# Two extra PSUM banks for the first eight projections of a hybrid mixer, and a modulation round whose end is cut into three steps

## The chip, the core and the metric

The kernel runs on one core of a Trainium2 chip. The metric is the device time of one execution in microseconds, from the first instruction to the last, as the median of several runs. The engines are named as in the profile: PE is TensorE (PEld its weight loads), DVE is VectorE, ACT is ScalarE, POOL is GpSimd, SP is the engine whose queue starts most DMAs.

## What is computed

Two blocks of two layers each, over 512 tokens of width 1024 with a context of 256 tokens, all in float32. The first block has a spatial gate and a two-way recurrent mixer in its first layer, a chunked matrix-memory mixer in its second, and a convolutional feed-forward part in both; what enters and leaves each part is scaled and shifted by a modulation, six vectors of 1024 for each layer, computed from a condition vector:

```python
def ada_mod(cvec, w, b):
    m = jax.nn.silu(cvec) @ w + b
    m = m.reshape(cvec.shape[:-1] + (6, D_MODEL))
...
```

The second block, run twice, is the hybrid mixer. One projection is split into many parts; q, k and v go through a short convolution, q and k are normalised, and four heads run a gated delta rule in chunks of 64 tokens in both directions; beside that a branch with a convolution of 31 taps, and two gates that mix the branches:

```python
def hybrid_mixer(h, w_in, qkv_conv_w, a_log, ...):
    proj = h @ w_in
    qkv, z_a, a_lg, b_lg, cf_val, cf_glu, z_b, gate_lg = jnp.split(proj, pts, axis=-1)
    qkv = jax.nn.silu(depthwise_conv_centred(qkv, qkv_conv_w))
    q = l2_normalize(q)
    k = l2_normalize(k)
    ...
    o_fwd = gated_delta_chunked(q, k, v, g[:, :, 0], beta[:, :, 0])
    o_bwd = flip(gated_delta_chunked(flip(q), flip(k), flip(v), ...))
    ...
    y = gate[:, :, 0] * y_a + gate[:, :, 1] * y_b
    return y @ w_out
```

## The kernel before

**Matmuls.** A float32 product is made of three fp32r matmuls for each of eight blocks of 128 rows: the weight tile is split into a high part `wh` (ACT, line 77) and a low part `wl` (DVE, line 78), the input likewise beforehand, and lines 329, 332 and 333 multiply high with high, high with low and low with high. One tile of 128 output columns over 512 tokens is thus 24 matmuls of 128x512 into one PSUM bank. Raw weights come by DMA into a ring of two buffers (`wr`); the split tiles have rings of three.

**PSUM banks.** An `Env` holds lists of bank numbers; `K.mm()` takes the next bank of `env.mm`, `K.ps()` the next of `env.ps`, each list in rotation. The main environment has 0 to 3 for `mm` and 4 to 7 for `ps`. A bank is one buffer: whoever takes it waits until the last reader of its previous content is done, in the order of the program's text.

**Strands.** `K.background` hands a generator to a list; at every `yield a, b` a strand is put off by a nominal time `b`, and `tick`, called between the matmuls of the main text, runs a step of each strand that is due. The text order so made is then reordered engine by engine by the framework's scheduler. Of the PE instructions of a step only the first is pinned behind the first of the step before it. The order on each engine is fixed when the program is built, and each engine runs its list in order.

**A hybrid.** `hybrid(K, CH, l, X)` first computes the gate rows (`gate_rows`, one tile of 24 matmuls), their cumulated sums `gc` along chunks (line 1809), and brings them into columns: `columns` transposes with four PE instructions each (line 1443) into a `ps` bank and copies (line 1446). There are four such columns, in this text order: `gcT`, `egT`, `beT`, `kdT`; then `eglT` (PE line 1833, copy line 1836). These five take consecutive banks of the main `ps` list: 5, 6, 7, 4, 5 in the first hybrid, and 6, 7, 4, 5, 6 in the second (counted from the program's calls of `K.ps()`).

After them in the text come the projections. `proj(h)` calls `gdn_proj`, which makes four tiles of 24 matmuls: k, q, v and za of head h, below called k0, q0, v0, za0, k1 and so on. The bank of k, q and v is read by one ACT instruction (line 1770) and four DVE instructions (line 1778). k and q are then passed through Silu (line 1996) and Square (line 1999), and the sum of squares goes through PE (`ps<-ones,qsq`, line 359, four instructions), DVE (line 349), POOL (line 351) and PE again (line 371). `pro` is the environment of the projections with the `mm` banks 0, 1 and 2, so that za0 takes the bank of k0, k1 that of q0, and so on. Two strands `head(0)` and `head(1)` have the `ps` banks 4, 5 and 6, 7; `head(0)` begins after `proj(0)`, `head(1)` after `proj(1)`. Then follow `cf_proj`, the strand `cf_conv`, `proj(2)`, `proj(3)` and the gates.

In the trace, the matmuls of all these tiles have lines 329, 332 and 333; the program's order, printed further down, tells the tiles apart by number.

**The modulation rounds.** `ada_steps` computes 2048 columns of the modulation in one round: eight steps, each with two or three loads into `wr` buffers (or, every third step, into the rings of `wh` and `wl`) and four matmuls of 32x512 (line 539), then a copy `adav` out of PSUM (DVE, line 545), four PE transposes (line 548) and two DVE additions (line 553). Its `ps` list is bank 3 alone. Round 0 runs at the start; five rounds run as one strand beside the strands of the recurrent mixer in the first layer, and then beside that mixer's output projection (`gemm_out`, weights `ab_w_out`).

Of the kernel before, what the change touches and what calls it, by code (L numbers as in the profile page):

```python
# [81 lines left out]
class Kern:  # L82
# [431 lines left out]
    def ada_steps(self, layer, rounds):  # L514
        nc = self.nc
        w = self.ins["ada_w"]
        if not hasattr(self, "mod"):
            self.mod = {}
            cs = self.const([P, KD, 32], name="csil")
            nc.gpsimd.memset(cs, 0.0)  # L520
            for i, key in enumerate(("c", "c_ctx")):
                nc.scalar.activation(cs[:, :, i], self.vt[key], AF.Silu)
            self.csil = cs
        if layer not in self.mod:
            self.mod[layer] = self.const([P, 2, 48], name="mod")
        mod = self.mod[layer]
        for r in rounds:
            ps = self.ps()
            for k in range(KD):
                if k % 3 < 2:  # L530
                    raw = self.wpool.tile([P, 2048], F32, tag="wr", bufs=2, name=self.nm("ar"))
                    raw = [raw[:, :1024], raw[:, 1024:]]
                else:
                    raw = [self.wpool.tile([P, 1024], F32, tag=t, bufs=3, name=self.nm("ar")) for t in ("wh", "wl")]
                for h in range(2):
                    c0 = 2048 * r + 1024 * h
                    self.lines[mybir.EngineType.SP] = nc.sync.dma_start(raw[h], w[layer, k * P:(k + 1) * P, c0:c0 + 1024]).ins
                for c in range(4):
                    m = nc.tensor.matmul(ps[32 * c:32 * c + 32, :], self.csil[:, k, :],  # L539
                                         raw[c // 2][:, 512 * (c % 2):512 * (c % 2) + 512], start=k == 0, stop=k == KD - 1)  # L540
                    if self.back and c == 0:
                        self.tc.keep_in_program_order(m)
                yield 860, ADL
            ev = self.p2(name="adav")
            nc.vector.tensor_copy(ev, ps)
            pt = self.ps()
            for q in range(4):
                nc.tensor.transpose(pt[:, q * P:(q + 1) * P], ev[:, q * P:(q + 1) * P], self.ident)
            self.free(ev)
            bias = self.vt[f"ada_b{layer}"]  # L550
            for i in range(2):
                src = pt.rearrange("p (q c x) -> p c q x", q=4, c=4)[:, :, :, i]
                nc.vector.tensor_tensor(mod[:, i, 16 * r:16 * r + 16].rearrange("p (c q) -> p c q", c=4), src,
                                        bias[:, 16 * r:16 * r + 16].rearrange("p (c q) -> p c q", c=4), ADD)
# [1227 lines left out]
def hybrid(K, CH, l, X):  # L1782
# [56 lines left out]
    pro = Env([0, 1, 2], [3], [], range(16, 24))  # L1839
    heads = [Env([], (4 + 2 * a, 5 + 2 * a), range(7 * a, 7 * a + 7), range(8 * a, 8 * a + 8)) for a in range(2)]  # L1840

    def proj(h):
        pre[h] = gdn_proj(K, l, h, X, w)

    def head(a):
        pads = CH.pads(K.p2)
        for h in (a, a + 2):
            while h not in pre:
                yield 0, 2000
            yield from gdn_head(K, CH, l, h, *pre.pop(h), gcT, ngT, beT, bkT, eglT, gcd, egd, Ya, pads)  # L1850
        K.free(*pads)

    K.env = pro
    K.gk = GKH
    for e in heads:
        K.lend([e], p=HP)
    for h in range(2):
        proj(h)
        K.background(heads[h], head(h), slow=SLG)
    cf_proj(K, l, X, w, U)  # L1860
    conv = cf_conv(K, l, U)
    K.background(pro, conv)
# [426 lines left out]
```

## Time and profile before

| what | value |
|---|---|
| median of 3 runs | 3439.56 us (3436.07 to 3442.67) |
| profiled execution | 3440.7 us, span 3439.0 us |
| PE busy | 3202.1 us, 93% of the span |
| DVE, ACT, POOL busy | 2121.8, 1272.1, 628.5 us |
| mean granted TensorE clock | 0.952 |
| chain that ended last, by engine | PE 78%, DVE 11%, ACT 3%, DMA 3% |

The first hybrid runs from about 2267 us to 2840 us of the span, the second from about 2846 us to the end; the five background rounds of the modulation lie between 400 and 770 us. A line of the timeline is: start, duration, engine, line, operation, output<-inputs, shapes, count, and in brackets the time for which the engine stood idle before it and whose end ended that. A matmul's duration overlaps the next one's, so a stretch is measured from start to start.

### The profile page before, as it was taken

Reading aid. Unit: us, or ns where it says so; the run is one execution under the profiler, and the core shown is the slowest. Engines: PE = TensorE matmul, PEld = TensorE weight load, DVE = VectorE, ACT = ScalarE, POOL = GpSimd, SP = SyncE. Lnnn points to the kernel's source line nnn. Section 1 sums busy time; section 2 is a strip of 40 time slices with the busy share of each in tenths; the row PEclk is TensorE's granted clock in tenths of the full one; section 3 lists DMA queues with packets and bytes.
Section 4 is the critical chain, followed back from the end, with each engine's and each line's share of the span. In section 5 each row is a group of like instructions: output and inputs, shape, how many; then the busy total and the mean of one; then the engine's idle time right before and its main releaser. Section 6 shows DMA issues by size and latency. Waiting matters only on the chain.

```text
span 3439.0 us, 62780 instructions
## 1 busy us (share of the span) xinstructions
PE 3202.1 (93%) x25436; PEld 2523.3 (73%) x25436; DVE 2121.8 (62%) x4341; ACT 1272.1 (37%) x2679; POOL 628.5 (18%) x762
## 2 busy tenths in 40 slices
PE   7999988989799999989988999979999898999998
PEld 5878767767588888868766788857767576766766
DVE  4444555645755555585765675667587656777665
ACT  4343343333442222355524332352333335234332
POOL 4111232311000000010010000005158000516600
PEclk9999998989899999999998999989999899999979
DMA  6432454441221222222222233232222253223233
GB/s 231 138 91 70 150 161 142 141 135 52 69 71 63 74 66 68 74 67 79 86 69 86 86 108 113 87 98 71 72 92 96 77 176 93 70 68 101 96 107 114
DMA packets 313573, 336.15 MB, mean 98 GB/s; under 512 B 26542, under 2 KB 259132, under 8 KB 313284
## 3 DMA queue, kind: packets, MB, share of 16 engines
q1 hardware_dynamic: 311172, 329.69, 30.2%
q8 instruction: 200, 3.28, 0.4%
q0 software_dynamic: 2112, 2.45, 0.3%
q14 instruction: 89, 0.73, 0.1%
HBM read 282.13 MB, written 49.94 MB: 97 GB/s over the span
## 4 chain that ended last, share of the span: by engine, by line
PE 78%; DVE 11%; ACT 3%; DMA 3%; issue 2%; POOL 2%; SPq 0%; DVEq 0%; POOLq 0%; ACTq 0%
PE mm L329 20%; PE mm L332 18%; PE mm L333 18%; PE ps L720 2%; PE ps L1176 2%; PE ps L729 2%; DVE cfa L1778 2%; PE ps L1121 1%; PE ps L539 1%; PE ps L371 1%; PE ps L2128 1%; DVE wl L78 1%; PE ps L1703 1%; PE ps L2115 1%; PE ps L2142 1%
## 5 line engine op out<-in xcount | busy, mean ns | idle before, releaser
L329 PE MATMUL mm<-hl,wh 128*128 128x512 f32 (+1 forms) x3296 | 1250.0, 383 | 42.8 <-DVE qkv L1778 15.0
L332 PE MATMUL mm<-hl,wh 128*128 128x512 f32 (+1 forms) x3296 | 1220.1, 371 | 1.1 <-DVE hl L468 0.8
L333 PE MATMUL mm<-hl,wl 128*128 128x512 f32 (+1 forms) x3296 | 1212.7, 370 | 0.0
L329 PEld LDWEIGHTS mm<-hl,wh 128*128 128x128 f32 x3296 | 628.2, 191 | 184.2 <-issue 38.2
L333 PEld LDWEIGHTS mm<-hl,wl 128*128 128x128 f32 x3296 | 628.3, 191 | 113.0 <-issue 2.5
L332 PEld LDWEIGHTS mm<-hl,wh 128*128 128x128 f32 x3296 | 630.0, 191 | 103.0 <-issue 2.8
L77 ACT ACTIVATE wh<-wr 128x512 fp32r<-128x512 f32 (+3 forms) x718 | 368.0, 562 | 694.1 <-PE mm L332 600.3
L78 DVE TENSOR_TENSOR wl<-wr,wh 128x512 fp32r<-128x512 f32 (+3 forms) x718 | 439.3, 645 | 221.5 <-ACT wh L77 205.2
L1356 DVE SCALAR_TENSOR_TENSOR cv<-mm,vecs,cv 128x441 f32<-128x441 f32 (+2 forms) x352 | 243.4, 692 | 93.6 <-ACT cv L1344 87.2
L1407 POOL MEMSET gwh<- 128x1024 f32 x3 | 2.9, 955 | 964.5 <-PE mm L332 964.5
L1778 DVE SCALAR_TENSOR_TENSOR cfa<-ld,vecs,cfa 128x497 f32<-128x497 f32 (+14 forms) x160 | 152.3, 952 | 18.1 <-ACT cfa L1772 16.0
L1944 POOL TENSOR_SCALAR tap<-ld,vecs 128x498 f32<-128x498 f32 (+4 forms) x80 | 146.5, 1831 | 50.7 <-DVE kq L2003 12.4
L1379 DVE TENSOR_TENSOR fy<-fy,mm 128x512 f32<-128x512 f32 x96 | 55.2, 577 | 126.2 <-PE mm L333 125.5
L1945 POOL TENSOR_TENSOR cfa<-cfa,tap 128x498 f32<-128x498 f32 (+4 forms) x80 | 119.1, 1489 | 5.5
L2120 ACT ACTIVATE u<-ps,beT 64x128 f32<-64x128 f32 x128 | 46.5, 363 | 152.6 <-DVE u L2119 151.6
L724 ACT ACTIVATE pad<-ps 128x256 f32<-128x256 f32 (+1 forms) x100 | 46.7, 467 | 150.9 <-PE ps L720 147.9
L1358 ACT ACTIVATE cv<-cv,vecs 128x256 f32<-128x256 f32 (+1 forms) x66 | 43.2, 654 | 132.7 <-DVE cv L1356 78.1
L351 POOL TENSOR_TENSOR rs<-var,mhalf 128x4 f32<-128x4 f32 (+1 forms) x26 | 29.0, 1115 | 287.7 <-DVE var L349 287.6
L406 PE MATMUL ps<-sq,one 128*128 128x512 f32 (+1 forms) x132 | 64.0, 625 | 18.9 <-ACT sq L376 17.2
L730 DVE TENSOR_TENSOR cut<-cut,ps 128x256 f32<-128x256 f32 x120 | 49.3, 415 | 51.4 <-PE ps L729 49.9
L1362 DVE TENSOR_TENSOR cv<-cv,mm 128x512 f32<-128x512 f32 x66 | 39.5, 599 | 65.5 <-ACT cv L1358 35.4
L2119 DVE TENSOR_SCALAR u<-ps,kdT 64x128 f32<-64x128 f32 x128 | 44.7, 349 | 52.1 <-PE ps L2115 41.8
(476 smaller groups left out, 4578.9 us busy)
## 6 DMA issues: line engine op xcount, KB each, us to landing
ar<-in_ada_w_dram SPq DMA_DIRECT2D x96, 512.0 KB, 4.8
wr<-in_ffn_up_dram SPq DMA_DIRECT2D x44, 1024.0 KB, 5.1
wr<-in_w_in_dram SPq DMA_DIRECT2D x28, 1024.0 KB, 5.3
ld<-sp SPq DMA_DIRECT2D x84, 256.0 KB, 2.9
wr<-in_w_in_dram SPq DMA_DIRECT2D x32, 512.0 KB, 3.8
xsp<-x SPq DMA_DIRECT2D x48, 256.0 KB, 2.0
x<-xsp SPq DMA_DIRECT2D x48, 256.0 KB, 3.9
wr<-in_ffn_down_dram SPq DMA_DIRECT2D x20, 512.0 KB, 3.5
```

Of the source, the lines that this page charges most:

```text
L77: nc.scalar.activation(h[:, q:e], src, AF.Copy)
L78: nc.vector.tensor_tensor(l[:, q:e], src, h[:, q:e].bitcast(F32), SUB)
L329: mm = nc.tensor.matmul(ps[:m, :n], wh[:, i, :m], H[:, :n], start=first and i == 0, stop=False)
L332: nc.tensor.matmul(ps[:m, :n], wh[:, i, :m], L[:, :n], start=False, stop=False)
L333: nc.tensor.matmul(ps[:m, :n], wl[:, i, :m], H[:, :n], start=False, stop=last and i == nk - 1)
L720: nc.tensor.matmul(ps[r, u * 64:u * 64 + 64], L[r, u], W[r, u], start=True, stop=True)
L729: nc.tensor.matmul(ps[r, u * 64:u * 64 + 64], X[r, u], Z[r, u], start=True, stop=True)
L1176: nc.tensor.matmul(ps[hs[h], d], lhsT(d, h), rhs(d, h), start=first and i == 0 and d == 0, stop=last and i == len(parts) - 1, skip_group_c ...
L1356: nc.vector.scalar_tensor_tensor(t3[:, ro, co], a3[:, ri, ci], tap(ky, kx, ff), t3[:, ro, co], MUL, ADD)
L1778: nc.vector.scalar_tensor_tensor(dst[:, a:b], src[:, a + o:b + o], taps[j], dst[:, a:b], MUL, ADD)
L1944: nc.gpsimd.tensor_scalar(x[:, a:b], src[:, a + o:b + o], taps[j], None, MUL)
L1945: nc.gpsimd.tensor_tensor(g[:, a:b], g[:, a:b], x[:, a:b], ADD)
```

## The change

The first eight projections of each hybrid get the banks 6 and 7 beside 0, 1 and 2: k0, q0, v0, za0, k1, q1, v1, za1 now take 0, 1, 2, 6, 7, 0, 1, 2. From `cf_proj` on the old environment holds again. In `ada_steps`, a `yield 0, 700` stands between the copy and the transposes of a round's end, and a `yield 450, 600` between the transposes and the additions, so that the end is three steps; the additions still share a step with the first loads and matmuls of the next round. No arithmetic changes. Behind line 546 line numbers are larger by 1 to 4 in the changed kernel.

```diff
--- before.py
+++ after.py
@@ -543,10 +543,12 @@
                 yield 860, ADL
             ev = self.p2(name="adav")
             nc.vector.tensor_copy(ev, ps)
+            yield 0, 700
             pt = self.ps()
             for q in range(4):
                 nc.tensor.transpose(pt[:, q * P:(q + 1) * P], ev[:, q * P:(q + 1) * P], self.ident)
             self.free(ev)
+            yield 450, 600
             bias = self.vt[f"ada_b{layer}"]
             for i in range(2):
                 src = pt.rearrange("p (q c x) -> p c q x", q=4, c=4)[:, :, :, i]
@@ -1850,13 +1852,15 @@
             yield from gdn_head(K, CH, l, h, *pre.pop(h), gcT, ngT, beT, bkT, eglT, gcd, egd, Ya, pads)
         K.free(*pads)
 
-    K.env = pro
+
+    K.env = Env([0, 1, 2, 6, 7], [3], [], range(16, 24))
     K.gk = GKH
     for e in heads:
         K.lend([e], p=HP)
     for h in range(2):
         proj(h)
         K.background(heads[h], head(h), slow=SLG)
+    K.env = pro
     cf_proj(K, l, X, w, U)
     conv = cf_conv(K, l, U)
     K.background(pro, conv)
```

Where instructions stand now, at three places (rows in the order in which the engine runs them; a line of `...` stands for the other rows of a matmul tile, or for rows of other strands).

PE in the first hybrid, before, from the last matmul of v0 (`mm_22284`) on; `mm_22325` is za0, `mm_22363` k1; `ps_22120`, `ps_22113` and `ps_22134` are the columns `egT`, `gcT` and `kdT`, `ps_22202` the sum of squares of k0, `ps_22147` is `eglT`, `ps_22211` the norm of k0 spread over rows:

```order
L333 MATMUL mm_22284<-hl_22025,wl_22279 128x512
L329 MATMUL mm_22325<-hl_21984,wh_22319 128x512
L332 MATMUL mm_22325<-hl_21985,wh_22319 128x512
...
L1443 MATMUL ps_22120<-ident_72,nat_22104 128x64 x4
...
L1443 MATMUL ps_22113<-ident_72,nat_22107 128x64 x4
L359 MATMUL ps_22202<-ones_77,qsq_22200 128x1
L1443 MATMUL ps_22134<-ident_72,nat_22101 128x64 x4
L359 MATMUL ps_22202<-ones_77,qsq_22200 128x1 x3
...
L329 MATMUL mm_22363<-hl_21984,wh_22357 128x512
...
L1833 MATMUL ps_22147<-egl_22097,ident_72 128x8 x8
L371 MATMUL ps_22211<-ident_72,rs_22209 128x128 x4
```

The same place, after:

```order
L333 MATMUL mm_22284<-hl_22025,wl_22279 128x512
L1445 MATMUL ps_22120<-ident_72,nat_22104 128x64 x4
L1445 MATMUL ps_22113<-ident_72,nat_22107 128x64 x4
L359 MATMUL ps_22202<-ones_77,qsq_22200 128x1 x4
L1835 MATMUL ps_22147<-egl_22097,ident_72 128x8 x8
L329 MATMUL mm_22325<-hl_21984,wh_22319 128x512
L1445 MATMUL ps_22134<-ident_72,nat_22101 128x64 x4
L332 MATMUL mm_22325<-hl_21985,wh_22319 128x512
...
L371 MATMUL ps_22211<-ident_72,rs_22209 128x128 x4
...
L329 MATMUL mm_22363<-hl_21984,wh_22357 128x512
```

The columns, the squares of k0 and `eglT`, which stood inside za0 and k1, now all stand ahead of za0's first matmul.

PE in the second hybrid, before: `mm_27321` is v0, `mm_27362` za0, `mm_27400` k1; `ps_27157` and `ps_27150` are `egT` and `gcT`, `ps_27239` the squares of k0, `ps_27184` `eglT`:

```order
L333 MATMUL mm_27321<-hl_27062,wl_27316 128x512
L329 MATMUL mm_27362<-hl_27021,wh_27356 128x512
...
L1443 MATMUL ps_27157<-ident_72,nat_27141 128x64 x4
...
L1443 MATMUL ps_27150<-ident_72,nat_27144 128x64 x4
L359 MATMUL ps_27239<-ones_77,qsq_27237 128x1 x2
L1443 MATMUL ps_27171<-ident_72,nat_27138 128x64 x4
...
L329 MATMUL mm_27400<-hl_27021,wh_27394 128x512
...
L1833 MATMUL ps_27184<-egl_27134,ident_72 128x8 x8
```

The same place, after:

```order
L333 MATMUL mm_27321<-hl_27062,wl_27316 128x512
L1445 MATMUL ps_27157<-ident_72,nat_27141 128x64 x4
L1445 MATMUL ps_27150<-ident_72,nat_27144 128x64 x4
L359 MATMUL ps_27239<-ones_77,qsq_27237 128x1 x4
L1835 MATMUL ps_27184<-egl_27134,ident_72 128x8 x8
L329 MATMUL mm_27400<-hl_27021,wh_27394 128x512
L1445 MATMUL ps_27171<-ident_72,nat_27138 128x64 x4
...
L371 MATMUL ps_27248<-ident_72,rs_27246 128x128 x4
...
L329 MATMUL mm_27362<-hl_27021,wh_27356 128x512
```

The same rows have moved ahead of the next projection, and that is k1; za0 now follows behind k1's first fourteen matmuls.

SP, the DMA starts around the first weights of the output projection, before: `ar` are weights of the modulation, `wr...<-in_ab_w_out` the slabs of the output projection, the rest serves the recurrent strands; `sp_9206<-y` writes out the result of the second strand:

```order
L537 DMA ar_9179<-in_ada_w_dram 128x1024 x2
...
L1033 DMA kq_9339<-rkv_809 128x2x128 x2
L1034 DMA cut_4302<-rkv_807 128x128 x2
L607 DMA ld_9254<-sp_8811 128x512
...
L304 DMA wr_9276<-in_ab_w_out_dram 128x6x256
L537 DMA ar_9397<-in_ada_w_dram 128x1024
L537 DMA ar_9398<-in_ada_w_dram 128x1024
L537 DMA ar_9488<-in_ada_w_dram 128x1024 x2
...
L304 DMA wr_9520<-in_ab_w_out_dram 128x6x256
L601 DMA sp_9206<-y_1637 128x512
```

The same place, after (`sp_9208<-y` is that write):

```order
L537 DMA ar_9068<-in_ada_w_dram 128x1024 x2
...
L1036 DMA cut_4302<-rkv_807 128x128 x2
L955 DMA cut_4301<-rkv_823 128x256
L304 DMA wr_9288<-in_ab_w_out_dram 128x6x256
L1035 DMA kq_9310<-rkv_809 128x2x128 x2
L609 DMA ld_9266<-sp_8768 128x512
...
L537 DMA ar_9386<-in_ada_w_dram 128x1024 x2
L537 DMA ar_9476<-in_ada_w_dram 128x1024 x2
...
L603 DMA sp_9208<-y_1637 128x512
...
L304 DMA wr_9493<-in_ab_w_out_dram 128x6x256
```

The first slab now stands ahead of two loads of strands, two more `ar` loads for the `wr` ring stand between the first slab and the second, and the second slab stands behind the write of `y`.

## Rows read from the trace of the kernel before

**Rows 1.** The page: span, and PE's line of section 1 (busy, share, instructions).
```profile
span 3439.0 us, 62780 instructions
PE 3202.1 (93%) x25436; PEld 2523.3 (73%) x25436; DVE 2121.8 (62%) x4341; ACT 1272.1 (37%) x2679; POOL 628.5 (18%) x762
```

**Rows 2.** Busy time by stretch: start:end, length, PE, PEld, DVE, ACT, POOL, PEclk.
```profile
560.00:700.00 140.00, 126.59 (x2507) 100.92 (x2505) 84.28 (x220) 50.50 (x156) 41.28 (x67) 0.90 0.48 146
2240.00:2420.00 180.00, 155.24 (x1142) 119.94 (x1141) 124.32 (x207) 72.17 (x112) 54.98 (x40) 0.91 0.28 85
```

**Rows 3.** PE's waits from 2240 to 2420: line <- releaser, total, times, longest.
```profile
PE mm L329 <- DVE qkv L1778: 7.6, 1, 7.6
PE ps L720 <- DVE W L730: 7.5, 3, 5.3
```

**Rows 4.** PE's timeline in the first hybrid, from the first matmul of za0.
```profile
2299.42 0.80 PE L329 MATMUL mm<-hl,wh 128*128 128x512 f32 x1 [7.56 <-DVE qkv L1778]
...
2304.84 0.48 PE L1443 MATMUL ps<-ident,nat 64*128 64x64 f32 x4
...
2306.83 0.46 PE L1443 MATMUL ps<-ident,nat 64*128 64x64 f32 x4
2307.22 0.38 PE L359 MATMUL ps<-ones,qsq 128*128 128x1 f32 x2
...
2307.93 0.83 PE L359 MATMUL ps<-ones,qsq 128*128 128x1 f32 x6
2308.62 0.48 PE L329 MATMUL mm<-hl,wh 128*128 128x512 f32 x1
...
2311.56 1.95 PE L1833 MATMUL ps<-egl,ident 64*128 64x8 f32 x16
```

**Rows 5.** ACT's timeline in the first hybrid: columns, Silu and Square of k0.
```profile
2298.28 2.55 ACT L1431 ACTIVATE nat<-gc 32x512 f32<-32x512 f32 x4
...
2302.14 0.63 ACT L1996 ACTIVATE qkv<-qkv 128x512 f32<-128x512 f32 x1
2302.81 0.63 ACT L1999 ACTIVATE qsq<-qkv 128x512 f32<-128x512 f32 x1
```

**Rows 6.** Busy time and granted clock by stretch around both waits (columns as Rows 2).
```profile
2299.40:2304.90 5.50, 5.48 (x13) 3.87 (x13) 4.64 (x7) 5.38 (x8) 0.00 (x0) 0.50 0.70 198
2304.90:2312.00 7.10, 7.10 (x43) 5.56 (x42) 2.14 (x10) 6.09 (x10) 0.67 (x1) 1.00 0.66 178
2878.80:2882.40 3.60, 3.60 (x10) 2.92 (x11) 3.56 (x6) 3.50 (x6) 0.00 (x0) 0.59 0.53 117
```

**Rows 7.** PE's timeline in the second hybrid, at the same place.
```profile
2878.76 0.80 PE L329 MATMUL mm<-hl,wh 128*128 128x512 f32 x1 [7.44 <-DVE qkv L1778]
...
2881.49 0.53 PE L329 MATMUL mm<-hl,wh 128*128 128x512 f32 x1
```

**Rows 8.** ACT's timeline in the second hybrid: Square of k0.
```profile
2882.15 0.64 ACT L1999 ACTIVATE qsq<-qkv 128x512 f32<-128x512 f32 x1
```

**Rows 9.** DVE's timeline in the second hybrid: E and eglT.
```profile
2890.09 0.79 DVE L2057 TENSOR_TENSOR E<-gcT,E 128x256 f32<-128x256 f32 x2 [2.95 <-DMA E<-sp]
2890.91 0.69 DVE L2058 TENSOR_TENSOR E<-E,big 128x512 f32<-128x512 f32 x1
...
2893.40 0.22 DVE L1836 COPY eglT<-ps 128x64 f32<-128x64 f32 x1
```

**Rows 10.** DVE's waits from 395 to 800, the one line on the modulation.
```profile
DVE mod L553 <- PE ps L548: 1.6, 2, 1.2
```

**Rows 11.** PE's timeline at 425: the four matmuls of one modulation step.
```profile
425.55 1.06 PE L539 MATMUL ps<-ar,csil 128*32 128x512 f32 x8
```

**Rows 12.** The SP queue's waits from 700 to 735.
```profile
SPq L304 <- PE ps L539: 5.3, 1, 5.3
```

**Rows 13.** The chain that ended last, 700 to 720: start, length, what.
```profile
706.36 6.58 DMA wr<-in_ab_w_out_dram
```

**Rows 14.** PE's timeline at 717.
```profile
717.23 1.01 PE L960 MATMUL ps<-blk,bon 128*128 128x2 f32 x4 [5.49 <-ACT bon L980]
```

## Prediction

> **What bounds the kernel now.** I read the page first, then busy time by stretch, then PE's waits, then the timelines at the places that the edits touch. PE is busy for 93% of the span [rows 1]. In the stretches of the change it has a little room: 90% at a granted clock of 0.90 where modulation steps run beside the recurrent strands, 86% at 0.91 where the first hybrid starts [rows 2]. So a microsecond counts in full if PE works or waits in it, and one on DVE, ACT or SP counts only if PE comes to wait for it.
>
> At the start of the first hybrid the largest wait of PE is one of 7.56 us, for the last DVE tap (line 1778) that reads k0's bank [rows 3, 4]: za0 wants bank 0, and k0 has not left it. The second hybrid has the same wait with 7.44 us [rows 7]. These two are what the new bank list can take away. In the modulation's background rounds PE has no wait on a round's end; DVE waits 1.6 us in all, twice, for the transposes of line 548 [rows 10].
>
> **First hybrid.** za0 now takes bank 6, k1 bank 7, q1 bank 0. But 6 and 7 are not empty: in the text order `egT` took 6 and `beT` 7, and a later taker waits for the last reader. The program's order, printed above, shows what comes of it: `egT`, `gcT`, the four squares of k0 (line 359) and `eglT` stand ahead of za0's first matmul, where before they stood inside za0 and k1. PE runs its list in order, so za0 starts when the last of them is done. When is that? The order on ACT and DVE up to the Square of k0 has not moved, and those two start from matmuls that have not moved either. So the Square ends at 2302.81 + 0.63 = 2303.44 as before [rows 5]. Behind it come line 359 with 0.38 + 0.83 = 1.21 and `eglT` with 1.95 [rows 4]: za0 starts at 2306.6, where before it started at 2299.42. That is 7.2 us later: the wait for a DVE tap has become a longer wait for a Square on ACT, which itself hangs on that tap.
>
> Not all of that is lost. `egT`, `gcT`, the squares and `eglT` (0.48 + 0.46 + 1.21 + 1.95 = 4.1 us) are then done, and before they lay inside the following matmuls. So 7.2 - 4.1 = 3.1 us remain.
>
> To that comes the clock. After the wait of 7.56 us the granted clock was 0.50 for 5.5 us, then 1.00 [rows 6]: twelve matmuls took 2304.84 - 2299.42 = 5.42 us at the low level and 2311.56 - 2308.62 = 2.94 us at the high one [rows 4], a loss of 2.5 us. In the second hybrid the clock came back earlier (0.59 over 3.6 us): six matmuls took 2881.49 - 2878.76 = 2.73 us against 2.94/2 = 1.47, a loss of 1.3 [rows 6, 7]. After the change PE is nearly idle from 2299.42 - 7.56 = 2291.9 to 2306.6 but for those 4.1 us (10.6 idle), so the fall comes again; I take 1.9 us, the mean of the two. Bounds: nothing, if the small instructions use up the low level, and 2.5 x 10.6/7.56 = 3.5 if the loss grows with the idle time. Sum: 3.1 - 2.5 + 1.9 = **+2.5 us**, between +0.6 and +4.1.
>
> The Trainium skill ("PSUM — Partial Sum Buffer", section "Engine vs sequencer instructions") says that TensorE can overlap a weight load with matmuls in flight, but that matmuls start and complete in program order. It speaks against the change: za0's weights may be in place, its matmul may not pass a waiting transpose. If matmuls could pass, za0 would start at 2291.9 and the result would be the first rival's.
>
> **Second hybrid.** The same rows have moved ahead of the next projection, which is now k1. The Square of k0 ends at 2882.15 + 0.64 = 2882.79 [rows 8]; with 1.21 and 1.95 again, k1 starts at 2885.95 instead of 2878.76: 7.2 later, 4.1 of it work, +3.1. The clock lost 1.3 and will lose 1.9 (between 0 and 2.5). Then za0, behind fourteen matmuls of k1, wants bank 6, which in this hybrid holds `eglT`: it waits for the copy of line 1836, which stands on DVE behind an `E` whose DMA comes at 2890.09, and its 0.79 and 0.69 [rows 9]. Right behind these the copy ends near 2891.9; PE gets there at about 2885.95 + 14 x 0.35 = 2890.9, a matmul costing 0.25 at the high and 0.45 at the low level. So 0 to 0.9, and I take 0.3 since the DMA may come earlier. Sum: 3.1 - 1.3 + 1.9 + 0.3 = **+4.0 us**, between +1.8 and +5.2.
>
> Later waits could give it back, if the other engines reach them at the old times. The largest one is 7.5 us of PE waiting for `W`, 5.3 at once [rows 3]; but `W` hangs on taps and copies that start from matmuls, and those move by the same 3 us. I take nothing from it; full absorption is a rival.
>
> From `cf_proj` on the old list holds. k1, q1 and v1 find their banks empty: PE showed no wait there before. Nothing for those.
>
> **The modulation rounds.** The two new yields cost no instruction. They move a round's transposes and additions some steps later and cut what one tick puts into PE's list. On PE there is nothing to win, since no wait on lines 548 or 553 stands there; DVE's 1.6 us [rows 10] hold up nobody that the trace shows. I take nothing for the cut itself, between -1.6 and 0.
>
> What does cost or bring something is that the rounds are put off: the yields add nominal times of 700, and of 450 and 600 ns, to a round; with the putting-off (700 and 600) stretched by the scheduler's factor `LF` of 2.5 that is 1.3 x 2.5 + 0.45 = 3.7 us a round, 18 us over five. Five rounds of eight steps lie between 400 and 770 us, about one step in 9 us, so two to three steps of 1.06 us [rows 11] leave the recurrent stretch and come to lie beside the output projection, which PE fills without gaps. PE's work is the same; what moves is the meeting at the first output weights. There the SP queue waits 5.3 us for a modulation matmul that must free a `wr` buffer [rows 12], the load then takes 6.58 us from 706.36 on [rows 13], ACT splits it, and since ACT runs its list in order the strands' `bon` comes late and PE idles 5.49 us at 717.23 [rows 14].
>
> After the change the first slab stands ahead of two other loads and behind earlier modulation matmuls, so its buffer should come free one step earlier; but the second slab stands behind two more `ar` loads and the write of `y`. Best case: all of the idle time goes, -5.49, with the -1.6 above -7. Worst case: one slab lies bare for its whole load, +6.6. The chain is a close race: PE's idle time hangs on the order of strands on ACT as much as on the load. I take **-1 us**, nearer to the middle than to either end, since the rows show both the gain and the danger.
>
> **Sum.** 2.5 + 4.0 - 1 = +5.5 us. The profiled execution took 3440.7 us, so 3446.2; the median of the runs is 1.1 below it, so **3445 us**. By the hybrids' bounds alone 3439.6 - 1 + 2.4 = 3441 to 3439.6 - 1 + 9.3 = 3448.
>
> **The rivals.**
> *A, the banks do free PE.* If za0 and k1 ran through, both waits and the clock's loss behind them would go: 7.56 + 7.44 + 2.5 + 1.3 = 18.8 us, some 3420. For it speak the two waits themselves. Against it stands the order: the takers of 6 and 7 are not done. It needs matmuls that pass waiting ones; chance 0.06. The Trainium skill's rule here ("Perfetto Trace Analysis", section "Matmuls") is that independent groups of matmuls should rotate through different banks so that emptying one overlaps the next; by it this rival would be the result. The rows show the wait that the rule means, and the order shows that the two added banks are in use.
>
> *B, the modulation wins more.* The idle 5.49 us at 717 and the 1.6 go, the hybrids lose their 6.5: 3439, chance 0.16.
>
> *C, slower by a bare slab.* The second slab of the output projection waits behind two more `ar` loads in a ring of two buffers, its 6.58 us lie bare, and PE stands: 6.5 + 6.6 - 1 = +12.1, some 3452. It decides once the slab lands later than the first slab's matmuls last. For it: those matmuls find modulation steps that hold the same ring for longer. Against it: the loads before it are only two. Chance 0.22.
>
> *D, the shift is absorbed.* The hybrids' 6.5 us vanish in the waits for `W` [rows 3]: 3438.6, chance 0.06.
>
> **How the numbers follow.** Forecast 0.50, A 0.06, B 0.16, C 0.22, D 0.06. A measurement of this kernel can tell about 0.2%, 6.9 us, from no change: slower begins at 3446.4. The forecast lies just below; of its own range 3441 to 3448 I count a third above the line, 0.17. So faster 0.06; same 0.33 + 0.16 + 0.06 = 0.55; slower 0.17 + 0.22 = 0.39. The range reaches down to -1.6 - 5.5 + 2.4 = -4.7, 3435, which takes in B and D, and up to 9.3 + 5 = +14.3, 3454, which takes in C. What lies outside is A and the corners of the bounds, together a little over one in ten.
>
> **What would show it.** Of the profile after: PE's wait for line 1778 is gone, and in its place PE stands before a transpose of line 1445 and before line 359, waiting for ACT, with za0 starting about 7 us later than before relative to v0's end, and the granted clock near 0.50 behind it; in the second hybrid the same, and za0 with a wait for `eglT`. If za0 starts right behind v0, A holds and I have misread the order. If the idle time at 717 is gone, B; if PE waits at lines 329 to 333 near 740 for a split of `ab_w_out`, C. If both hybrids' PE starts late but the second's end is not, D. I am wrong in the sum also if the clock stays down much longer than the 5.5 us shown, or if the Square comes earlier because ACT's columns go ahead of it in another rhythm.

## The result and the profile after

The changed kernel takes 3471.93 us in the median (3463.24 to 3477.81), before 3439.38 us; the ratio is 1.0091 with a 95% interval of 1.0077 to 1.0105, so it is some 31 us slower (26 to 36). The forecast was 3445 and its range ended at 3454. The profiled execution took 3470.81 us.

To see where the time went, the two traces are laid side by side by the count of matmuls of lines 329, 332 and 333: the 7061st such matmul stands at the same point of the work in both. Four stretches are used from here on: **the recurrent stretch**, from the 1091st to the 1401st (before: 378.40 to 853.47 us; modulation rounds and the start of the output projection lie in it), **the start of the first hybrid**, 7061st to 7401st, **the rest of it**, 7401st to 8561st, and **the start of the second**, 8561st to 8801st. The view is the busy time by stretch, its columns as in [rows 2]: start:end, length, then PE, PEld, DVE, ACT, POOL, then PE's granted clock. Of before:

```profile
378.40:853.47 475.07, 422.84 (x7629) 331.42 (x7628) 264.44 (x678) 170.90 (x504) 122.14 (x213) 0.92 0.43 133
2268.96:2391.68 122.72, 108.67 (x710) 87.71 (x709) 86.77 (x143) 57.91 (x89) 33.76 (x26) 0.93 0.28 82
2391.68:2857.61 465.93, 439.01 (x3111) 322.58 (x3110) 320.06 (x616) 165.40 (x351) 154.03 (x104) 0.95 0.32 100
2857.61:2938.18 80.57, 73.02 (x402) 59.40 (x401) 51.28 (x98) 47.14 (x70) 8.22 (x10) 0.96 0.38 111
```

The same four of after:

```profile
379.38:861.79 482.41, 425.90 (x7652) 334.80 (x7651) 262.39 (x680) 171.64 (x505) 120.40 (x213) 0.91 0.42 131
2281.36:2410.91 129.55, 112.83 (x709) 91.81 (x708) 86.95 (x143) 57.99 (x89) 32.95 (x26) 0.90 0.27 78
2410.91:2880.56 469.65, 439.02 (x3112) 322.18 (x3110) 319.02 (x616) 165.29 (x351) 150.38 (x104) 0.94 0.31 99
2880.56:2967.42 86.86, 76.74 (x402) 62.96 (x400) 50.68 (x98) 47.01 (x70) 7.47 (x10) 0.90 0.36 103
```

The losses are 7.3, 6.8, 3.7 and 6.3 us. (The 4 us in the third hang on one late `u` of a head, and the experiments show that this stretch varies by as much with an unchanged order.) Some 4 more lie near 1900 us, where PE waits 4.6 us for a convolution tap of DVE instead of 2.3. In the hybrids' starts PE's idle time (length less busy) has grown from 14.1 to 16.7 and from 7.6 to 10.1 us, and the clock has fallen.

PE's waits at the start of the first hybrid, after (line <- releaser, total, times, longest), which answer to [rows 3]:

```profile
PE ps L1445 <- ACT nat L1433: 8.3, 2, 7.7
PE ps L722 <- DVE W L732: 7.5, 3, 5.3
...
PE ps L359 <- ACT qsq L2003: 1.9, 1, 1.9
```

The wait for line 1778 is gone; in its place PE waits 8.3 us for `nat`, the ACT rows that the columns are transposed from, and 1.9 for the Square. The timeline of PE there, from the end of the first wait to za0's first matmul, answers to [rows 4]:

```profile
2312.08 0.69 PE L1445 MATMUL ps<-ident,nat 64*128 64x64 f32 x4 [7.71 <-ACT nat L1433]
2313.37 0.69 PE L1445 MATMUL ps<-ident,nat 64*128 64x64 f32 x4 [0.61 <-ACT nat L1433]
2315.98 1.87 PE L359 MATMUL ps<-ones,qsq 128*128 128x1 f32 x8 [1.92 <-ACT qsq L2003]
2317.78 3.58 PE L1835 MATMUL ps<-egl,ident 64*128 64x8 f32 x16
2321.28 0.79 PE L329 MATMUL mm<-hl,wh 128*128 128x512 f32 x1
```

What holds the Square is ACT's own list, in after:

```profile
2310.65 0.21 ACT L1815 ACTIVATE egl<-gc 64x8 f32<-64x8 f32 x1 [2.21 <-DVE gc L1811]
2310.77 2.55 ACT L1433 ACTIVATE nat<-gc 32x512 f32<-32x512 f32 x4
2313.34 1.28 ACT L2000 ACT_TABLE_LOAD   x1
2314.63 0.63 ACT L2000 ACTIVATE qkv<-qkv 128x512 f32<-128x512 f32 x1
2315.29 0.63 ACT L2003 ACTIVATE qsq<-qkv 128x512 f32<-128x512 f32 x1
```

k0's last tap ends on DVE at 2311.12 + 0.74 = 2311.86; the Silu (line 2000) starts 2.8 us later, since four `nat` pieces, which waited for DVE's `gc`, and an ACT_TABLE_LOAD of 1.28 us stand ahead of it.

`egT`, `gcT`, the squares and `eglT` stand in a row ahead of za0, as the program's order said. But each of the small ones takes longer than in [rows 4]: the squares 1.87 us, `eglT` 3.58 instead of 1.95. The busy time by stretch says why:

```profile
2304.40:2312.10 7.70, 0.02 (x1) 0.02 (x1) 7.58 (x13) 5.43 (x11) 0.00 (x0) 0.69 0.26 69
2312.10:2326.90 14.80, 12.28 (x51) 10.73 (x52) 8.12 (x21) 11.59 (x15) 1.01 (x1) 0.50 0.61 160
2326.90:2334.00 7.10, 7.10 (x35) 5.99 (x35) 2.21 (x5) 2.99 (x5) 0.73 (x2) 0.94 0.00 0
```

The granted clock stays at 0.50 (the lower of the two levels, 1.2 GHz) for 14.8 us, against 5.5 us in [rows 6]; in them PE does transposes, squares and `eglT` with two short waits between, and then the first matmuls of za0. The second hybrid has the same picture: waits of 7.59, 0.61 and 1.92 us, and a granted clock of 0.61 over the 14 us behind them. The predicted wait of za0 for `eglT` did not show there.

The modulation's side, PE's waits from 380 to 735 us, after:

```profile
PE ps L722 <- DVE cut L732: 8.6, 8, 3.3
PE ps L967 <- DVE gn L976: 6.6, 4, 2.2
PE ps L1123 <- DVE kq L1104: 4.1, 3, 1.5
```

The same waits of before:

```profile
PE ps L720 <- DVE cut L730: 6.0, 5, 3.4
...
PE ps L1121 <- DVE kq L1102: 3.4, 2, 2.0
...
PE ps L965 <- DVE gn L974: 1.7, 1, 1.7
```

The wait of 5.49 us for `bon` [rows 14], on which the prediction set its eye, is gone, and still the stretch is longer.

### The profile page after: what moved, and what is told of

Its sections match the earlier page's. It is cut to its first block, busy times and chain, and to the rows that moved or that the text cites. A ratio compares the mean times of both kernels' runs of the same rounds, so it can differ in the third digit from the quotient of the medians.

```text
span 3468.8 us, 62771 instructions
## 1 busy us (share of the span) xinstructions
PE 3213.5 (93%) x25436; PEld 2532.5 (73%) x25436; DVE 2117.7 (61%) x4341; ACT 1270.5 (37%) x2679; POOL 618.3 (18%) x762
## 4 chain that ended last, share of the span: by engine, by line
PE 78%; DVE 12%; ACT 4%; DMA 3%; issue 2%; POOL 2%; SPq 0%; DVEq 0%; POOLq 0%; ACTq 0%
PE mm L329 20%; PE mm L332 18%; PE mm L333 18%; DVE cfa L1780 2%; PE ps L731 2%; PE ps L722 2%; PE ps L1178 2%; PE ps L1123 1%; PE ps L371 1%; DVE wl L78 1%; PE ps L2132 1%; PE ps L539 1%; PE ps L406 1%; PE ps L1705 1%; PE ps L2119 1%
## 5 line engine op out<-in xcount | busy, mean ns | idle before, releaser
L351 POOL TENSOR_TENSOR rs<-var,mhalf 128x4 f32<-128x4 f32 (+1 forms) x26 | 27.6, 1062 | 289.5 <-DVE var L349 289.4
L2132 PE MATMUL ps<-u,kt 64*128 64x128 f32 x224 | 60.4, 357 | 18.1 <-DVE u L2123 9.9
```

Source lines behind the costliest of these rows:

```text
L2132: nc.tensor.matmul(pS[:, q], kt[half(p), 128 * i:128 * i + 128], u2[half(p)], start=True, stop=True)
```

## The experiments

The table has for each kernel the ratio to before with its interval, and the lengths of the four stretches in one profiled execution, in us, with PE's idle time and granted clock in the recurrent stretch. A single execution varies, so the ratio says what an edit is worth, and the stretches where to look.

| kernel | ratio (95%) | recurrent (idle, clock) | 1st start | rest | 2nd start |
|---|---|---|---|---|---|
| before | | 475.1 (52, 0.92) | 122.7 | 465.9 | 80.6 |
| after | 1.0091 (1.0077 to 1.0105) | 482.4 (57, 0.91) | 129.6 | 469.7 | 86.9 |
| e1_banks | 1.0051 (1.0032 to 1.0070) | 469.1 (51, 0.93) | 129.1 | 476.3 | 87.7 |
| e2_steps | 1.0041 (1.0024 to 1.0057) | 484.3 (56, 0.91) | 122.8 | 466.3 | 80.8 |
| e3_cut_only | 1.0000 (0.9986 to 1.0015) | 470.1 (51, 0.93) | 122.3 | 474.8 | 80.5 |
| e4_free_banks | 1.0002 (0.9989 to 1.0015) | 472.3 (50, 0.92) | 121.5 | 472.7 | 83.8 |
| e5_put_off | 1.0023 (1.0010 to 1.0035) | 476.9 (57, 0.92) | 121.2 | 467.6 | 79.6 |
| e6_earlier | 1.0054 (1.0037 to 1.0070) | 487.4 (55, 0.92) | 122.2 | 469.5 | 81.9 |
| e7_norms_behind_k1 | 1.0060 (1.0044 to 1.0077) | 473.3 (49, 0.91) | 114.7 | 488.0 | 84.1 |
| e8_columns_behind_k1 | 1.0079 (1.0059 to 1.0099) | 475.9 (54, 0.92) | 119.6 | 483.1 | 85.7 |
| e9_first_yield | 1.0004 (0.9993 to 1.0015) | 474.9 (59, 0.93) | 122.8 | 466.3 | 80.5 |
| e10_second_yield | 1.0046 (1.0032 to 1.0060) | 491.1 (57, 0.89) | 122.4 | 469.5 | 80.4 |
| e11_cut_same_time | 1.0021 (1.0007 to 1.0035) | 479.1 (51, 0.90) | 122.6 | 473.8 | 81.0 |
| e12_columns_in_4_5 | 1.0028 (1.0015 to 1.0041) | 475.5 (53, 0.92) | 125.9 | 474.9 | 86.6 |
| e13_second_put_off | 1.0022 (1.0012 to 1.0033) | 474.4 (57, 0.93) | 122.9 | 466.4 | 80.5 |
| e14_second_clock_on | 0.9989 (0.9981 to 0.9998) | 480.2 (50, 0.91) | 121.4 | 470.8 | 79.8 |
| e15_first_longer | 1.0042 (1.0029 to 1.0055) | 484.9 (54, 0.90) | 122.3 | 474.7 | 81.3 |
| e16_both_without_600 | 0.9974 (0.9961 to 0.9987) | 462.4 (46, 0.93) | 122.6 | 473.6 | 81.3 |

### The two halves apart

**e1_banks** is the hunk in `hybrid` alone.

```diff
-    K.env = pro
+    K.env = Env([0, 1, 2, 6, 7], [3], [], range(16, 24))
...
+    K.env = pro
     cf_proj(K, l, X, w, U)
```

> The bank list alone, the modulation as before. Theory 1 (both halves of the change cost, each where its trace shows it): the two late starts of the hybrids cost 6.7 and 6.3 us, and the later u on DVE in the middle of the first hybrid 4 us more if it comes from the banks: 13 to 17 us slower, 3452 to 3457. Rival 1 (the sum on record for the banks was right, and the modulation is nearly all of it): +6.5, about 3446.

Measured: 3460.02 against 3442.38 us, +17.6 by the medians (11 to 24 by the interval). The two starts lose 6.3 and 7.1 us:

```profile
2262.65:2391.71 129.06, 112.36 (x709) 91.28 (x708) 86.72 (x143) 57.77 (x89) 32.96 (x26) 0.90 0.27 78
2867.96:2955.66 87.70, 75.78 (x402) 62.67 (x400) 51.15 (x98) 48.61 (x71) 7.75 (x10) 0.88 0.36 102
```

Theory 1 holds, the sum on record (+6.5) does not. The remaining 4 us of the 17.6 can't be placed with one profile. The recurrent stretch is left alone by this edit (its order there is before's), and took 469.1 us in this execution against 475.1: that is the noise of one profile.

**e2_steps** is the hunk in `ada_steps` alone.

```diff
             nc.vector.tensor_copy(ev, ps)
+            yield 0, 700
             pt = self.ps()
...
             self.free(ev)
+            yield 450, 600
```

> The two yields alone, the banks as before. Theory 1: 7 us of the loss lie between 400 and 830 us, and the other order of DVE's taps near 1895 us, 3 to 4 us, comes from the yields too: +10 to +15, 3450 to 3454. Rival 1: with the banks at only 6.5, the yields have to account for 23 or more, 3462. Rival 2 (the yields cost nothing, as on record): 3438.

Measured: 3457.49 against 3442.38, +15 by the medians (8 to 20 by the interval). Theory 1 holds here too. Both halves thus cost, 0.51% and 0.41%, and their sum is, within the intervals, the 0.91% of the whole change. The recurrent stretch takes 484.27 us, and the late DVE tap near 1900 us (4.6 us of PE's waiting instead of 2.3) comes with this half:

```profile
379.30:863.57 484.27, 428.23 (x7653) 335.42 (x7651) 261.70 (x679) 171.38 (x504) 120.55 (x213) 0.91 0.42 131
```

The six profiled executions with before's order in that stretch (before, e1, e4, e7, e8, e12) took 469 to 476 us there, with 49 to 54 us of idle time of PE and clocks of 0.91 to 0.93.

### The banks

**e4_free_banks** keeps the longer list and takes the tenants out of banks 6 and 7: the columns and `eglT` use 4 and 5 in turn.

```diff
+    kept, K.env.ps = K.env.ps, deque((4, 5))
     gcT = columns(K, [(gcn, n)], "gcT")
...
     nc.vector.tensor_copy(eglT, ps[:, :64].rearrange("p (r c) -> p r c", r=8))
+    K.env.ps = kept
...
-    K.env = pro
+    K.env = Env([0, 1, 2, 6, 7], [3], [], range(16, 24))
```

> The same longer bank list, but the five columns ahead of it take the banks 4 and 5 in turn, so that 6 and 7 are empty. Theory 1 (the tenants of 6 and 7 are what turned the gain into a loss): za0 starts right behind v0, the waits of 7.5 us of PE at line 1778 go in both hybrids and the half clock behind them too: 15 to 19 us faster, 3420 to 3425. Rival (the engines behind PE are late anyway, and the wait only moves to k1 or a column): within 5 us of before.

Measured: 1.0002, no difference. The loss of e1 is gone, and so is the wait of za0; but the gain of 15 to 19 us did not come. In the second hybrid one can see where it went. PE works from 2868 us with two short waits (0.2 and 0.4 us), idles for 3.36 us up to 2886.31, and then has the low clock:

```profile
2868.00:2884.00 16.00, 14.34 (x65) 10.77 (x63) 11.69 (x19) 14.20 (x20) 0.00 (x0) 1.00 0.38 97
2884.00:2886.30 2.30, 0.00 (x0) 0.00 (x0) 0.23 (x1) 2.25 (x5) 0.00 (x0) 0.94 0.87 137
2886.30:2903.00 16.70, 15.44 (x62) 13.66 (x63) 6.05 (x19) 8.02 (x12) 3.35 (x5) 0.50 0.62 177
```

Its timeline at the end of that idle time:

```profile
2886.31 1.87 PE L359 MATMUL ps<-ones,qsq 128*128 128x1 f32 x8 [3.36 <-ACT qsq L2002]
```

40 matmuls behind v0 (one projection and 16 of the next one's 24) go by almost without waiting, then the squares of k0 stand in PE's list, and the Square on ACT is not ready. PE's idle time there is down (5.2 us in the stretch against 7.6), and the clock eats it: 0.50 for 16.7 us, and the stretch is 3.3 us longer than before all the same. ACT's timeline shows why:

```profile
2881.10 1.28 ACT L1999 ACT_TABLE_LOAD   x1
2882.39 0.63 ACT L1999 ACTIVATE qkv<-qkv 128x512 f32<-128x512 f32 x1
2883.04 1.28 ACT L1431 ACT_TABLE_LOAD   x1
2884.34 1.27 ACT L1431 ACTIVATE nat<-tmp 32x512 f32<-32x512 f32 x2
2885.63 0.63 ACT L2002 ACTIVATE qsq<-qkv 128x512 f32<-128x512 f32 x1
```

k0's taps are done before 2880 us, but ACT runs the columns' `nat` pieces and two table loads of 1.28 us ahead of the Square, one load and two pieces of them between the Silu and the Square. More banks move the meeting and do not bring this chain forward. Whether the Silu and the Square ahead of the `nat` pieces in ACT's list would, no run tested.

**e12_columns_in_4_5** is the control: the columns in 4 and 5, the old list.

> The control for e4_free_banks: the columns take banks 4 and 5 in turn, and the first projections have the old list 0, 1, 2. Theory: nothing is won or lost by that alone at the start of a hybrid; PE waits 7.5 us for line 1778 as before, and the time is within 5 us of before. Rival: the columns in two banks cost time of their own, 5 us or more, and the longer list of e4_free_banks made up for that.

Measured: 1.0028, some 10 us slower; the rival holds. With two banks the columns move ahead of za0, and PE waits there for ACT as in the change itself:

```profile
2304.08 0.68 PE L1443 MATMUL ps<-ident,nat 64*128 64x64 f32 x4 [8.28 <-ACT nat L1431]
```

e12 and e4 differ by the longer list alone: with free banks it brings about 9 us (1.0028 against 1.0002, each against before in its own series of runs), about what the columns' move to 4 and 5 costs.

**e7_norms_behind_k1** is e4 with the squares and norms of head 0 behind k1's last matmul on PE; **e8_columns_behind_k1** has the columns there too.

```diff
-    for h in range(2):
-        proj(h)
+    gs = [gdn_proj(K, l, h, X, w) for h in range(2)]
+    next(gs[0]), next(gs[0])
+    next(gs[1])
+    for h in range(2):
+        if h:
+            next(gs[1])
+        pre[h] = next(gs[h])
         K.background(heads[h], head(h), slow=SLG)
```

(`gdn_proj` is a generator here; it stops behind the tile k and behind za, and issues the squares and norms after that, the first PE instruction of each of head 0's tied behind the last matmul issued.)

> As e4_free_banks, and the squares and norms of the first head's k and q are held behind the last matmul of k1 on PE. Theory 1 (what e4 won at za0 it lost at the squares of k0, where PE waited 2.0 and 3.4 us and then ran at the half clock): both go, 5 to 12 us faster than before. Rival (the first head's chain is what bounds the hybrid, and starting its norms later costs what PE wins): as e4, within 3 us of before, or slower.

> As e7_norms_behind_k1, and the five columns and eglT too come behind k1 (banks 4, 5 and 6 in turn). Theory 1: the wait of 1.5 us for the columns goes as well, 8 to 16 us faster than before, and PE is busy without a gap from k0 to v1. Rival: the chain of the first head is late by as much, with waits of PE for W, u and S in its place; within 3 us of before, or slower.

Measured: 1.0060 and 1.0079, 21 to 27 us slower. The rival holds, and clearly. In e7 the start is 8 us shorter than before, with 8.3 us of idle time of PE instead of 14.1, and the rest of the first hybrid 22 us longer:

```profile
2268.54:2383.19 114.65, 106.37 (x613) 85.99 (x612) 83.75 (x141) 59.27 (x89) 29.87 (x23) 0.93 0.30 88
2383.19:2871.19 488.00, 455.91 (x3208) 331.30 (x3206) 318.77 (x618) 166.97 (x353) 153.07 (x107) 0.92 0.30 95
```

(About 100 small instructions have moved from the first stretch into the second; the two have the same number of PE instructions in sum as before, 3821.) Together the two take 602.7 us against before's 588.7. It is not idle time: PE idles 40.4 us in the two together against 41.0, and the waits for the heads' `S` came to 10.2 us in the second stretch, against 12.9 in before. Busy time has grown by 14.6 us, at a clock of 0.92 in the second stretch against 0.95. So the rival is right in the time, but that the heads' chain is what costs it is not shown; and one profile can't part the cost from that stretch's own variation, which e3_cut_only (below) puts at 9 us.

### The modulation rounds

**e3_cut_only** has the two yields with no time in them (`yield 0, 0` twice).

> The round's end cut into three steps, but with no nominal time at either cut. If the cost of the yields is the time by which they put the modulation off, PE's filler in the recurrent stretch stays and the kernel is within 2 us of before. If the cut itself costs (transposes and additions in steps of their own), it is 5 us or more slower.

Measured: 1.0000. Cutting a round's end into steps costs nothing; it also hardly changes the order: in the recurrent stretch 31 of the 678 places in DVE's list hold another instruction than in before, in e2 438. On the rest of the first hybrid this execution took 474.8 us, where before took 465.9 with the same order of instructions: that stretch varies by 9 us by itself.

**e5_put_off** and **e6_earlier** move the rounds in time and cut nothing.

```diff
-                yield 860, ADL
+                yield (860, ADL) if k < KD - 1 else (1310, ADL + 1300)
```

and, for e6_earlier, `ADL = 2600` in place of 2800.

> The modulation rounds put off by the same nominal time as in the change, in one piece behind a round's eighth step, and the end of a round not cut. Theory 1 (modulation matmuls are filler in the recurrent stretch, and what they are put off by is the loss): as the two yields, 10 to 15 us slower, with about three steps fewer ahead of 728 us of the span, some 5 us more idle time of PE and 10 us or more of further half clock between 380 and 860 us. Rival (the loss came from the particular order that the cuts made): within 3 us of before.

> The other way: each modulation step is put off by 2600 instead of 2800, which makes the five rounds some 20 us of nominal time shorter. Theory 1 (filler): two or three steps more lie in the recurrent stretch, PE idles less there: 3 to 11 us faster. Rival (the strands have no room for more, and the steps delay them as much as they fill): within 3 us of before, or slower.

Measured: 1.0023 and 1.0054. Later costs some 8 us and earlier some 17. PE's idle time is longer in both (57 and 55 us against 49 to 54 with before's order). The rule that modulation matmuls are filler, and that each one put off is a loss, fails: up to the 1150th matmul, some 25 us into the output projection, e6 has run all 40 modulation steps, before 38, and e6 is slower.

**e9, e10, e13, e14, e15 and e16** part the two yields into their numbers. The first number of a yield moves the nominal clock on for all strands, the second puts off this strand alone (times `LF` = 2.5).

```diff
 e9   yield 0, 700        (no second yield)
 e15  yield 0, 1300       (no second yield)
 e10  (no first yield)    yield 450, 600
 e13  (no first yield)    yield 0, 600
 e14  (no first yield)    yield 450, 0
 e16  yield 0, 700        yield 450, 0
```

> The first new yield alone (nothing, then 700, between the copy out of PSUM and the transposes). e6_earlier was slower, so filler alone does not explain the loss. Theory 2 (it is the order on PE, ACT and DVE in the recurrent stretch: before has a good one, and any other meets more waits for gn, cut and hl and more half clock): slower by 5 to 15 us although only about half of the time is put off. Theory 1 (the loss follows the time put off): half of the 11 us that the two yields lose there, 5 us.

> The second new yield alone (450, then 600, between the transposes and the additions). Theory 2: as e9_first_yield, 5 to 15 us slower, with no rule that the parts add up to the 15 us of both. Theory 1: half of 11 us, and both halves together 11.

> The second yield with its second number alone (0, then 600). The first number of a yield moves the nominal clock on for all strands, the second puts off the modulation alone. Theory 3 (the 450 does the harm: every strand's next step comes due earlier against the main text): within 3 us of before. Theory 4 (putting the additions into a later step does it, with the matmuls of the next round behind them): 10 to 16 us slower.

> The second yield with its first number alone (450, then 0). Theory 3: 10 to 16 us slower, with PE's half clock from 380 to 860 us near 100 us against 65 to 78. Theory 4: within 3 us of before.

> The first yield alone with 1300 in place of 700, so that a round is put off by about as much as by both yields. If putting the modulation off costs nothing (as e9_first_yield says), within 3 us of before. If it costs in proportion to the time, and e9 was too small to show it, 8 to 12 us slower, as e5_put_off.

> Both yields, the second with 450 and then 0. If the parts add up (first yield +1, the 450 alone -3, the 600 alone +8), this is within 4 us of before, 3436 to 3443, and the 600 was the costly part. If what counts is the whole interleaving that comes out, the parts tell nothing of it: 5 to 15 us slower, as e2_steps and e10_second_yield.

Measured: e9 1.0004, e15 1.0042, e10 1.0046, e13 1.0022, e14 0.9989, e16 0.9974. Theory 3 falls (e14 is even a little faster), theory 4 holds in sign with about half the size and agrees with e16. e9 came out below both of its expectations (+1 us against 5 or more), and e16 faster than both of its own. Nothing adds up: 450 alone -3 us and 600 alone +8 by the medians, 450 with 600 +19; 700 alone +1, but 1300 in the same place +17; and 700 with 450, from which a sum would give -2, is 7 to 9 us faster than before. Between e2 and e16 only the 600 differs, and with it 0.7% of the time (each against before in its own series), though both have run 36 modulation steps up to the 1150th matmul. The recurrent stretch of e10 and of e16:

```profile
380.26:871.40 491.14, 433.85 (x7693) 342.67 (x7692) 263.49 (x681) 170.73 (x507) 121.55 (x213) 0.89 0.41 129
```

```profile
379.62:842.06 462.44, 415.96 (x7669) 327.79 (x7667) 265.81 (x679) 171.21 (x506) 120.47 (x213) 0.93 0.44 137
```

PE does the same work in both but for 24 small instructions. (e10's profile is of its slowest execution.) In e16 it idles 46 us and has a clock of 0.93, in e10 57 us and 0.89: of the 28.7 us between them 11 are idle time, and 18 are busy time, nearly the same matmuls at the lower level for longer. Idle time alone does not decide: e9 idles 59 us and is no slower than before, at a clock of 0.93. And no one wait stands for it. In e9 the two largest are those for `cut` and `gn`, larger than in after,

```profile
PE ps L721 <- DVE cut L731: 10.7, 7, 3.3
PE ps L966 <- DVE gn L975: 7.7, 4, 2.3
```

while in e16 `gn` is down and `kq` up:

```profile
PE ps L1123 <- DVE kq L1104: 7.9, 5, 2.7
...
PE ps L967 <- DVE gn L976: 1.8, 3, 1.4
```

**e11_cut_same_time** has both yields as in the change, and an eighth step that is put off by so much less (`410, ADL - 1300`).

> Both yields with their times, and the eighth step of a round put off by that much less (410 and 1500 instead of 860 and 2800), so that a round as a whole takes the nominal time of before. Theory 1: no time is put off in sum, within 3 us of before. Theory 2: the order in the recurrent stretch is another one all the same, 5 to 15 us slower, with PE's idle time from 380 to 860 us at 54 us or more against 50 to 52.

Measured: 1.0021, 8 us slower, at a clock of 0.90 and with 51 us of idle time. Theory 2 holds in the time; its number for the idle time was wrong, since here the clock carries the loss alone.

What follows: neither the cut (e3) nor the time put off (e2 and e16, e5 and e6) predicts the cost. What is left is the order of the four recurrent strands and the modulation that comes out of the yields; this is argued by exclusion and not shown by itself, and an order that is much changed need not cost (e9: 494 such places in DVE's list, and 1.0004). Which feature of the order makes PE lose its clock more often is not settled; the traces show the loss spread over the 475 us, in waits for `cut`, `gn`, `kq` and `hl` whose shares change from program to program. Part of it lies beyond: in e2, e6 and e15 PE waits 4.3 to 4.7 us for the DVE tap near 1900 us, in before, e1, e3 and e16 2.2 to 2.4. In e2, e6 and e15 DVE's list has the taps and weight splits there in another order, though the edit is more than 1000 us earlier.

e16_both_without_600 beats both kernels: 0.9974 (0.9961 to 0.9987), 4 to 13 us faster than before. It has the hunk of the change in `ada_steps`, with 0 in place of the 600, and the old banks. It is the best of sixteen kernels, picked after the fact from one series of 12 runs.

## Why the prediction was wrong, step by step

**The place of the waits: right.** The order on PE was read rightly. za0 waits for `egT`, `gcT`, the squares and `eglT`, the wait for line 1778 is gone, and rival A, a gain of 18.8, was rightly given little. One link was misread: the Square was said to hang on k0's tap. The tap ended at 2299.4 in before, and the Silu began at 2302.14 [rows 5], behind the `nat` pieces and a table load (1.28 us from 2300.85) on ACT. The time of the Square came out right all the same, since ACT's order did not move. The Trainium skill's "PSUM — Partial Sum Buffer", section "Engine vs sequencer instructions", has matmuls start in program order; the trace agrees, za0's first matmul (2321.28) follows `eglT` (2317.78). The Trainium skill's "Perfetto Trace Analysis", section "Matmuls", asks for a rotation through banks so that emptying one overlaps the next group; e4 shows banks that are free and projections that do overlap the emptying of k0's bank. That was worth about 9 us against e12 and nothing against before (1.0002), since the columns' move to banks 4 and 5 costs 10 us and PE waits for k0's squares instead.

**The clock in the hybrids: mis-sized.** The working took za0 to start at 2306.6 in before's time. Its start at 2321.28 lies, with the 12.5 us by which after was late already (7151st matmul: 2291.2 before, 2303.7 after), at 2308.8. The step that failed is "I take 1.9 us", the mean of what the clock cost before, with 3.5 as its bound. It took the small instructions at their durations of [rows 4], where they ran at the full clock. In after they ran at the low level: the squares 1.87 instead of 1.21, `eglT` 3.58 instead of 1.95. They did not use up the low level either, as the lower bound supposed: it stayed for 14.8 us. With the measured 6.8 and 6.3 us in place of 2.5 and 4.0, the clock's term is 6.8 - 3.1 + 2.5 = 6.2 in the first hybrid and 6.3 - 3.1 + 1.3 = 4.5 in the second, against 1.9 in both. e1 lost 6.3 and 7.1 us at the two places. The idle time was the smaller part: 2.7 and 2.6 us more of it than before, against 4.2 and 3.7 us more busy time.

**No absorption: right, as far as it can be told.** The waits for `W` in the first hybrid stayed at 7.5 us in all.

**The modulation: wrong in sign and size.** -1 was predicted, with bounds of -7 and +6.6; e2 measured +15 by the medians (8 to 20). The step that failed is "PE's work is the same; what moves is the meeting at the first output weights". The wait for `bon` at 717, on which it was built, did go, as rival B wished, and the bare slab of rival C did not come: the longest wait of the output projection's matmuls is 3.2 us, for `hl`, a split of the input and not of the weights, where in before it was 2.0. Two modulation steps, of the forecast two to three, moved behind the 1150th matmul. The loss is not in one place: up to that matmul e2 has lost 5.1 of its 9.2 us and after 1.2 of its 7.3, although those two steps are still to come, and the rest is lost behind it, where the steps are made up. What in the new order costs the time stays open. The reordering of the strands there was in the program's order for all to see, and was not costed at all, since no single row had a price for it. e5 and e6 show that no price per step put off would have served: both directions cost. The bound should have allowed for an interleaving that is worse all along the stretch; one per cent of clock or of waiting in 475 us is 5 us. It is a rival that was missing.

**The sum.** +31 is 0.51% from the banks and 0.41% from the yields, some 13 us of the former at the two starts, where 6.5 were predicted.

## What to carry to other kernels

Before a bank is added to a rotation, find out who holds it: here it cost 0.51% with tenants in it and was worth about 9 us with the tenants elsewhere, which by itself cost as much. Then follow the chain to its next reader, and read the list of the engine that it waits for; here other work on ACT held the Square, and not the tap. When small matmuls come to stand behind a wait, cost them at the low clock, and the wait by what the clock costs behind it, which here was more than the idle time added. In a program that interleaves strands by due times, a changed time reorders hundreds of instructions; its price can't be summed from the few waits in view, and both signs should be in the range until a run has told.

## What the runs showed of the hardware

The low clock held over 14.8 us in which PE was busy for 12.28 us, with transposes, 128x1 and 64x8 matmuls, two short waits and the first wide matmuls; in before it was back after 5.5 us of wide matmuls [rows 6].

One program varies over executions by more than most of these edits are worth: before ran from 3432.28 to 3457.95 us in the 28 runs shared with e1 to e4, and the rest of the first hybrid took 465.9 us in one program and 474.8 in another with the same order on PE and DVE, at clocks of 0.95 and 0.93:

```profile
2384.99:2859.79 474.80, 447.16 (x3112) 328.01 (x3110) 319.74 (x616) 165.18 (x351) 152.22 (x104) 0.93 0.31 98
```

That row is of e3; PE's idle time in it is 27.6 us against 26.9 before, so the 9 us are nearly all clock.
